# The last pair of a QKV projection done quad by quad, a later load of x, and casts of w on other engines

## The chip, the cores and the metric

The kernel runs on one core of one Trainium2 chip. The metric is the device time of one execution in microseconds (us), from before the first instruction to after the last store has landed; the time of a kernel is the median of its runs.

## The reference

One matrix product of fp32 matrices, split by columns into three outputs:

```
batch, seq, hidden = 16, 512, 768
qkv = np.matmul(x, w_qkv)            # (8192 x 768) @ (768 x 2304)
q, k, v = qkv[..., :hidden], qkv[..., hidden:2*hidden], qkv[..., 2*hidden:]
return np.stack([q, k, v], axis=0)   # 3 x 16 x 512 x 768, fp32
```

## The kernel before

**Pairs, quads and the remainder.** The 8192 rows of x are worked off in 32 pairs p of 2 x 128 rows. The 2304 columns of w are two groups q = 0, 1 of 1024 columns and 256 left over (`w_rem`). A quad (p, q) is an output tile `o` of 2 x 128 rows by 2 x 512 columns, that is four parts c11, c12, c21, c22 of 128 x 512. It is made by a scheme of seven block products instead of eight (Winograd's): products 1 and 2 are bf16 matmuls on the rounded x (`xb`) and `b1`, products 3 to 7 are matmuls on sums of x (`s`) and sums of w (`t`, `b22`). One product is three matmuls of 128 x 512. They go into three PSUM banks of the quad, x, y and z, and `do(u, n)` (L219) issues product n with what leaves the bank after it:

- 1 starts bank x, and ScalarE copies it to c11; 2 fills bank z, and VectorE adds it to c11.
- 6 adds onto bank x, ScalarE copies it to c12; 7 adds onto x, ScalarE copies it to c22; 4 adds onto x, ScalarE copies it to c21.
- 5 starts bank y; after 7, VectorE adds y to c22; 3 adds onto y, VectorE adds y to c12.

So products 6, 7 and 4 each add onto a bank that ScalarE must have read first, and product 3 onto one that VectorE must have read.

**Order.** The order on every engine is the program's own (`manual_schedule`). From pair 2 on, `two(a, b, early)` (L274) works on the two quads a and b of one pair in turn: a1 b1 a2 a6 b2 b6 a5 a7 b5 b7 a4, the remainder, b4 a3 b3, with stores of whole quads. `early` issues the next pair's transposition on VectorE (L123), its rounding (L174) and sums (L182 to L186) on GpSimd, and the load of x for the pair after that, half on SyncE's queue, half on ScalarE's. The last pair, p = 31, goes through `two_last` (L308): the same order, with stores by rows and parts, and the remainder's two rows at the very end, each copied by ScalarE (L333) and stored from ScalarE's queue (L335).

**The start.** x of pairs 0, 1 and 2 and all of w are loaded on SyncE's queue, in the order x0, `w_rem`, x1, w(0,0), x2, w(0,1), w(1,0), w(1,1), x3, where w(q,c) is the block of 512 columns c of group q and comes in two halves h of 3 x 512 per partition. Pairs 0 and 1 are done by plain bf16 matmuls: `rem(0)`, `rem(1)` and then `block(q, c, w, cast_next)` (L373), four blocks of 24 matmuls, each with its four PSUM banks copied by ScalarE (L390), and the casts of the next block's w issued by `cast_next` among these copies. Between `block(0, 0)` and `block(0, 1)` stand, for pair 2, the transposition by TensorE (L168), copies out of PSUM by VectorE (L138) and ScalarE (L139), the rounding and sums on GpSimd, and on VectorE the four sums of w for q = 0 (`sum_w`, L106) and a cast (L420). After the blocks VectorE makes the four sums for q = 1 (L427, again L106) and a cast (L428), and then the transposition for pair 3 (L123).

**Tiles that are used again.** The tag "big" has eight buffers for the `o` tiles and for the halves of w of q = 1. Quad (2, 1), quad b of the first pair in `two`, takes the buffer of the half (1, 0, 1) of w, which the last sum of q = 1 reads. Up to eight DMAs are under way at a time: each waits until the one eight before it, in the order of their issue, has landed.

Of the kernel before, what the change touches and what calls it, by code (L numbers as in the profile page):

```python
# [10 lines left out]
def kernel(  # L11
# [20 lines left out]
    nc = tc.nc  # L32
    P = 128
# [6 lines left out]
    KH = KT // 2  # L40
    KC = K // 4
    NP = M // (2 * P)
    CB = 512
    REM = N3 - 4 * CB
# [5 lines left out]
    ident = mybir.ActivationFunctionType.Identity  # L50
# [21 lines left out]
    b1 = [w_pool.tile([P, KT, CB], bf16, name=f"b1_{q}") for q in range(2)]  # L72
# [11 lines left out]
    stage = {}  # L84

    def load_blocks(q, c):
        if q == 0:
            t = tq_pool.tile([P, KT, CB], fp32, name="st0", tag="tq")
            for h in range(2):
                load_w(t[:, h * KH:(h + 1) * KH], h * KH, KH, Q_OFF[q] + c * CB, CB)  # L90
            stage[q, 0, c], stage[q, 1, c] = t[:, :KH, :], t[:, KH:, :]
        else:
            for h in range(2):
                t = big_pool.tile([P, KH, CB], fp32, name="st1", tag="big")
                load_w(t[:], h * KH, KH, Q_OFF[q] + c * CB, CB)
                stage[q, h, c] = t[:]
# [15 lines left out]
    def load_x(p, other):  # L112
        xin[p] = xin_pool.tile([P, 2 * P // G, KC], fp32, name="xin")
        t = xin[p]
        rows = x_flat[p * 2 * P:(p + 1) * 2 * P, :].rearrange("(g b) k -> b g k", b=G)
        for n in range(2):
            for h in range(2):
                i = 2 * h + n
                (nc.sync, other)[h].dma_start(t[i * G:(i + 1) * G], rows[:, :, i * KC:(i + 1) * KC])
# [52 lines left out]
    def round_x(p):  # L172
        xb[p] = xb_pool.tile([P, KT, 2 * P], bf16, name="xb")
        nc.gpsimd.tensor_copy(out=xb[p][:], in_=xf[p][:])  # L174
# [18 lines left out]
    def quad(p, q):  # L193
        u = Quad()
        u.p, u.q = p, q
        u.o = big_pool.tile([P, 2, 2 * CB], fp32, name="o", tag="big")
        u.x = u.y = u.z = None
        return u

    def product(u, n, ps, start):  # L200
        t1, t2, t3, t4 = ts[u.q]
        if n <= 2:
            h = (n - 1) * KH
            lhs = [xb[u.p][:, h + j, :P] for j in range(KH)]
            rhs = [b1[u.q][:, h + j, :] for j in range(KH)]
        else:
            k, t = {3: (4, b22[u.q][:]), 4: (0, t4), 5: (1, t1), 6: (2, t2), 7: (3, t3)}[n]
            lhs = [sr[u.p][:, k, j, :] for j in range(KH)]
            rhs = [t[:, j, :] for j in range(KH)]
        for j in range(KH):  # L210
            nc.tensor.matmul(  # L211
                ps[:], lhs[j], rhs[j],
                start=(start and j == 0), stop=(j == KH - 1), skip_group_check=True,
            )

    def bank():
        return ps_pool.tile([P, CB], fp32, name="ps")

    def do(u, n):  # L219
        c11, c12 = u.o[:, 0, :CB], u.o[:, 0, CB:]  # L220
        c21, c22 = u.o[:, 1, :CB], u.o[:, 1, CB:]
        if n == 1:
            u.x = bank()
            product(u, 1, u.x, True)
            nc.scalar.activation(c11, u.x[:], ident)  # L225
        elif n == 2:
            u.z = bank()
            product(u, 2, u.z, True)
            nc.vector.tensor_tensor(c11, c11, u.z[:], op=add)  # L229
        elif n == 6:  # L230
            product(u, 6, u.x, False)
            nc.scalar.activation(c12, u.x[:], ident)  # L232
        elif n == 5:
            u.y = bank()
            product(u, 5, u.y, True)
        elif n == 7:
            product(u, 7, u.x, False)
            nc.scalar.activation(c22, u.x[:], ident)  # L238
            nc.vector.tensor_tensor(c22, c22, u.y[:], op=add)  # L239
        elif n == 4:  # L240
            product(u, 4, u.x, False)
            nc.scalar.activation(c21, u.x[:], ident)  # L242
        elif n == 3:
            product(u, 3, u.y, False)
            nc.vector.tensor_tensor(c12, c12, u.y[:], op=add)  # L245
# [4 lines left out]
    def store_quad(u):  # L250
        if u.q == 0:
            nc.sync.dma_start(rows_of(0, u.p, 0, H), u.o[:, :, :H])
            nc.sync.dma_start(rows_of(1, u.p, 0, 2 * CB - H), u.o[:, :, H:])
        else:
            part = 2 * H - Q_OFF[1]
            nc.sync.dma_start(rows_of(1, u.p, H - part, H), u.o[:, :, :part])
            nc.sync.dma_start(rows_of(2, u.p, 0, H), u.o[:, :, part:])

    def rem_row(p, r, ps):
        for j in range(KT):  # L260
            nc.tensor.matmul(  # L261
                ps, xb[p][:, j, r * P:(r + 1) * P], w_rem[:, j, :],
                start=(j == 0), stop=(j == KT - 1), skip_group_check=True,
            )
# [30 lines left out]
    def store_cols(u, r, lo, hi, eng):  # L295

        c = Q_OFF[u.q] + lo
        end = Q_OFF[u.q] + hi
        while c < end:
            n = min(end, (c // H + 1) * H)  # L300
            row = (2 * u.p + r) * P
            eng.dma_start(
                out_flat[c // H, row:row + P, c % H:c % H + n - c],
                u.o[:, r, c - Q_OFF[u.q]:n - Q_OFF[u.q]],
            )
            c = n

    def two_last(a, b):  # L308

        do(a, 1)  # L310
        do(b, 1)
        do(a, 2)
        do(a, 6)
        do(b, 2)
        do(b, 6)
        do(a, 5)
        do(a, 7)
        do(b, 5)
        do(b, 7)
        store_cols(b, 0, 0, CB, nc.sync)  # L320
        do(a, 4)
        store_cols(a, 1, 0, 2 * CB, nc.sync)
        do(b, 4)
        store_cols(b, 1, 0, 2 * CB, nc.scalar)
        do(a, 3)
        store_cols(a, 0, 0, 2 * CB, nc.sync)
        do(b, 3)
        store_cols(b, 0, CB, 2 * CB, nc.sync)
        for r in range(2):
            ps = bank()  # L330
            rem_row(a.p, r, ps[:, :REM])
            o = or_pool.tile([P, 2, REM], fp32, name="orem")
            nc.scalar.activation(o[:, 0, :], ps[:, :REM], ident)  # L333
            row = (2 * a.p + r) * P
            nc.scalar.dma_start(out_flat[1, row:row + P, R_OFF - H:R_OFF - H + REM], o[:, 0, :])  # L335


    zero = w_pool.tile([P, CB], bf16, name="zero")
# [14 lines left out]
    o0 = [quad(p, 0) for p in range(2)]  # L353
    load_blocks(1, 0)
    load_blocks(1, 1)
    load_x(3, nc.sync)
    o1 = [quad(p, 1) for p in range(2)]

    def busy(n):
# [2 lines left out]
        for _ in range(n):  # L362
            nc.tensor.matmul(ps[:], zero[:, :P], zero[:], start=True, stop=True)

    def cast(q, h, c, w, eng):

        dst = w[:, h * KH:(h + 1) * KH, :]
        if eng is nc.scalar:
            eng.activation(dst, stage[q, h, c], ident)
        else:  # L370
            eng.tensor_copy(out=dst, in_=stage[q, h, c])

    def block(q, c, w, cast_next):  # L373


        ps = [bank() for _ in range(4)]
        for h in range(2):
            for n in range(4):
                p, r = divmod(n, 2)
                for j in range(h * KH, (h + 1) * KH):  # L380
                    nc.tensor.matmul(  # L381
                        ps[n][:], xb[p][:, j, r * P:(r + 1) * P], w[:, j, :],
                        start=(j == 0), stop=(j == KT - 1), skip_group_check=True,
                    )
                if h == 0:
                    continue
                if r == 0:
                    cast_next(p)
                o = (o0, o1)[q][p]
                nc.scalar.activation(o.o[:, r, c * CB:(c + 1) * CB], ps[n][:], ident)  # L390
                if c == 1 and r == 1:
                    store_quad(o)

    act, dve = nc.scalar, nc.vector
# [7 lines left out]
    rem(0)  # L402
    turn_bf16(1)
    rem(1)
    cast(0, 0, 0, b1[0], dve)
    cast(0, 1, 0, b1[0], dve)
    bt0 = bt_pool.tile([P, KT, CB], bf16, name="bt")
    bt1 = bt_pool.tile([P, KT, CB], bf16, name="bt")

    def cast_next(q, c, w):  # L410

        return lambda h: cast(q, h, c, w, act)

    block(0, 0, b1[0], cast_next(0, 1, bt0))
    turn_fp32(2)
    round_x(2)
    sums_x(2)
# [1 line left out]
        sum_w(0, n)  # L419
    dve.tensor_copy(out=b22[0][:], in_=stage[0, 1, 1])  # L420
    block(0, 1, bt0, cast_next(1, 0, b1[1]))
    block(1, 0, b1[1], cast_next(1, 1, bt1))
    block(1, 1, bt1, lambda h: None)
    t_1 = [tq_pool.tile([P, 2, KH, CB], f32r, name=f"t_1{n}", tag="tq") for n in range(2)]
# [5 lines left out]
    for p in range(2, NP):  # L430
        def early():
            if p + 1 < NP:
                transpose(p + 1)
                round_x(p + 1)
                sums_x(p + 1)
            if p + 2 < NP:
                load_x(p + 2, nc.scalar)

        if p < NP - 1:
            two(quad(p, 0), quad(p, 1), early)  # L440
        else:
            two_last(quad(p, 0), quad(p, 1))


# [28 lines left out]
```

## Time and profile before

| what | value |
|---|---|
| median of 4 runs (lowest to highest) | 369.63 us (369.53 to 369.74) |
| the profiled execution: its time | 369.58 us |
| its span, first to last instruction | 367.8 us |
| TensorE busy, share of the span | 359.0 us, 98% |
| VectorE, ScalarE, GpSimd busy | 62%, 51%, 50% |
| TensorE clock granted, mean | 0.997 |
| the chain that ended last, by engine | TensorE 90%, VectorE 4%, DMA 2%, issue 1%, ScalarE 1% |
| one pair in `two`, on that chain | 1.33 us remainder + 9.54 us quads |
| HBM traffic | 32.24 MB read, 75.50 MB written |

How to read it: "TensorE busy" counts matmuls whose ends are modelled, so what counts is not the 98% but the stretches in which a matmul waits. A timeline row gives the start, the duration, the engine (PE is TensorE, PEld its weight loads, DVE VectorE, ACT ScalarE, POOL GpSimd; a q behind it means the engine's queue, which issues DMAs), the line, the operation, the tiles out<-in and their shape, how many instructions are merged, and in brackets how long the engine stood idle before it and what ended that.

### The profile page before, as it was taken

What the parts mean: (1) busy time and instruction counts of PE and PEld (TensorE: products, weight loads), DVE (VectorE), ACT (ScalarE), POOL (GpSimd) and SP (SyncE); (2) the same over time, 40 slices, a digit from 0 to 9 for tenths busy, and PEclk for the clock granted to TensorE, in tenths of its full rate; (3) what the DMA queues carried; (4) which work ended last, traced back from release to release, by engine and by line L of the source; (5) the groups of instructions that cost most, each with busy time, mean ns of one, the idle gap of its engine ahead of it and who ended that gap; (6) DMA issues with size and microseconds to landing.
All of it is one profiled execution on the core that took longest, in us unless ns stands there. A gap on an engine that the chain in (4) does not pass through costs nothing.

```text
span 367.8 us, 5180 instructions
## 1 busy us (share of the span) xinstructions
PE 359.0 (98%) x1791; PEld 246.5 (67%) x1791; DVE 229.1 (62%) x233; ACT 186.1 (51%) x308; POOL 184.5 (50%) x188
## 2 busy tenths in 40 slices
PE   7999899999999999999999999999999999999994
PEld 3544667667766667776666776666777676677663
DVE  2399876655576665567665557666556766555732
ACT  4498444545544455454454554455545444445442
POOL 1049374456654356664445665444665544566510
PEclk9999999999999999999999999999999999999998
DMA  8999988888998888998888899988899888899776
GB/s 285 390 373 342 325 292 272 278 298 272 305 322 278 270 292 273 309 311 290 273 282 295 272 308 305 286 279 290 280 299 313 293 268 283 283 284 311 259 272 242
DMA packets 80122, 108.09 MB, mean 294 GB/s; under 512 B 4704, under 2 KB 59872, under 8 KB 80096
## 3 DMA queue, kind: packets, MB, share of 16 engines
q1 hardware_dynamic: 64288, 95.96, 79.4%
q10 hardware_dynamic: 15808, 11.80, 10.1%
q8 instruction: 14, 0.23, 0.3%
q14 instruction: 12, 0.10, 0.1%
HBM read 32.24 MB, written 75.50 MB: 293 GB/s over the span
## 4 chain that ended last, share of the span: by engine, by line
PE 90%; DVE 4%; DMA 2%; issue 1%; ACT 1%; SPq 0%; ACTq 0%; DVEq 0%
PE ps L211 77%; PE ps L261 11%; DVE t L106 3%; DMA xin<-in_x_dram 2%; PE ps L381 1%; DVE b L420 0%; PE ps L168 0%; PE ps L157 0%; ACT orem L333 0%; SPq L82 0%; ACT o L225 0%; ACT xc L139 0%; DVE xf L138 0%; SPq L134 0%; ACTq L335 0%
## 5 line engine op out<-in xcount | busy, mean ns | idle before, releaser
L211 PE MATMUL ps<-t,s 128*128 128x512 f32 x720 | 194.4, 412 | 1.2 <-ACT o L225 1.2
L211 PEld LDWEIGHTS ps<-t,s 128*128 128x128 f32 x720 | 133.1, 188 | 34.0 <-ACT o L225 1.7
L174 POOL CAST xb<-xf 128x1536 bf16<-128x1536 f32 x30 | 45.4, 1514 | 162.9 <-DVE xf L123 141.7
L123 DVE STREAM_TRANSPOSE xf<-xin 128x1536 f32<-128x1536 f32 x29 | 87.2, 3006 | 1.5 <-DMA xin<-in_x_dram 1.3
L211 PE MATMUL ps<-b,xb 128*128 128x512 bf16 x360 | 88.1, 381 | 0.0
L245 DVE TENSOR_TENSOR o<-o,ps 128x512 f32<-128x512 f32 x60 | 41.3, 688 | 61.5 <-PE ps L211 61.4
L239 DVE TENSOR_TENSOR o<-o,ps 128x512 f32<-128x512 f32 x60 | 41.2, 689 | 55.0 <-ACT o L238 55.0
L211 PEld LDWEIGHTS <-xb 128*128 128x128 bf16 x360 | 30.5, 98 | 44.5 <-issue 15.5
L238 ACT ACTIVATE o<-ps 128x512 f32<-128x512 f32 x60 | 36.0, 600 | 46.7 <-PE ps L211 46.7
L225 ACT ACTIVATE o<-ps 128x512 f32<-128x512 f32 x60 | 35.8, 597 | 46.3 <-PE ps L211 42.2
L232 ACT ACTIVATE o<-ps 128x512 f32<-128x512 f32 x60 | 35.8, 599 | 44.0 <-PE ps L211 43.3
L261 PE MATMUL ps<-w_rem,xb 128*128 128x256 bf16 x384 | 47.7, 273 | 0.5 <-DVE w_rem L400 0.4
L211 PE MATMUL ps<-b,s 128*128 128x512 f32 x180 | 46.5, 393 | 0.0
L261 PEld LDWEIGHTS <-xb 128*128 128x128 bf16 x384 | 34.9, 98 | 13.2 <-issue 8.9
L229 DVE TENSOR_TENSOR o<-o,ps 128x512 f32<-128x512 f32 x60 | 38.1, 683 | 2.0 <-PE ps L211 2.0
L211 PEld LDWEIGHTS ps<-b,s 128*128 128x128 f32 x180 | 33.8, 188 | 8.0
L242 ACT ACTIVATE o<-ps 128x512 f32<-128x512 f32 x60 | 35.9, 598 | 4.8 <-PE ps L211 0.4
L183 POOL TENSOR_TENSOR s<-s,xf 128x384 fp32r<-128x384 f32 x30 | 31.1, 1037 | 2.3
L186 POOL TENSOR_TENSOR s<-xf,s 128x384 fp32r<-128x384 f32 x30 | 32.1, 1070 | 0.0
L182 POOL TENSOR_TENSOR s<-xf 128x384 fp32r<-128x384 f32 x30 | 31.9, 1064 | 0.0
L184 POOL TENSOR_TENSOR s<-xf 128x384 fp32r<-128x384 f32 x30 | 31.7, 1058 | 0.0
L271 ACT ACTIVATE orem<-ps 128x512 f32<-128x512 f32 x31 | 18.6, 598 | 23.3 <-PE ps L261 23.3
(39 smaller groups left out, 115.2 us busy)
## 6 DMA issues: line engine op xcount, KB each, us to landing
out_dram<-o SPq DMA_DIRECT2D x62, 768.0 KB, 5.8
out_dram<-o SPq DMA_DIRECT2D x63, 256.0 KB, 4.7
xin<-in_x_dram SPq DMA_DIRECT2D x60, 192.0 KB, 6.7
xin<-in_x_dram ACTq DMA_DIRECT2D x56, 192.0 KB, 5.7
out_dram<-orem SPq DMA_DIRECT2D x31, 256.0 KB, 2.4
st<-in_w_qkv_dram SPq DMA_DIRECT2D x8, 768.0 KB, 13.9
xin<-in_x_dram SPq DMA_DIRECT2D x3, 768.0 KB, 7.4
str<-in_w_qkv_dram SPq DMA_DIRECT2D x1, 768.0 KB, 6.1
```

What stands on the lines that cost most here:

```text
L123: nc.vector.transpose(t[:].rearrange("p j (g b) -> p g j b", b=G), xin.pop(p)[:].rearrange("p g (a j) -> p g j a", a=G),)
L174: nc.gpsimd.tensor_copy(out=xb[p][:], in_=xf[p][:])
L186: g.tensor_tensor(s[:, 4], a12, s[:, 2], op=sub)
L211: nc.tensor.matmul(ps[:], lhs[j], rhs[j], start=(start and j == 0), stop=(j == KH - 1), skip_group_check=True,)
L225: nc.scalar.activation(c11, u.x[:], ident)
L229: nc.vector.tensor_tensor(c11, c11, u.z[:], op=add)
L232: nc.scalar.activation(c12, u.x[:], ident)
L238: nc.scalar.activation(c22, u.x[:], ident)
L239: nc.vector.tensor_tensor(c22, c22, u.y[:], op=add)
L242: nc.scalar.activation(c21, u.x[:], ident)
L245: nc.vector.tensor_tensor(c12, c12, u.y[:], op=add)
L261: nc.tensor.matmul(ps, xb[p][:, j, r * P:(r + 1) * P], w_rem[:, j, :], start=(j == 0), stop=(j == KT - 1), skip_group_check=True,)
```

## The change

It has four parts.

1. `two_last` is replaced by `last`: the two quads of pair 31 one behind the other, each as 1 2 6 5 7, one row of the remainder, 4 3, each part of `o` stored as soon as it is complete. The second row of the remainder stands inside quad b, so the last product is b3 and the last store the c12 part of b.
2. `load_x(3)`, four DMAs on SyncE's queue, moves from before the first stores to behind `block(0, 1)`, which issues the stores of the two q = 0 quads of pairs 0 and 1.
3. The cast of w(0,0) for `block(0, 0)`: of each half's three rows of 512, VectorE casts two and ScalarE the third, instead of VectorE all three.
4. The cast of the second half of w(0,1) for `block(0, 1)` moves from ScalarE to GpSimd, ahead of GpSimd's work for pair 2.

```
-    def two_last(a, b):
...
+    def last(a, b):
+        p = a.p
+        def rem_stored(r):
             ps = bank()
-            rem_row(a.p, r, ps[:, :REM])
+            rem_row(p, r, ps[:, :REM])
             o = or_pool.tile([P, 2, REM], fp32, name="orem")
             nc.scalar.activation(o[:, 0, :], ps[:, :REM], ident)
...
+        for r, u in enumerate((a, b)):
+            do(u, 1)
+            do(u, 2)
+            store_cols(u, 0, 0, CB, nc.sync)
+            do(u, 6)
+            do(u, 5)
+            do(u, 7)
+            rem_stored(r)
+            store_cols(u, 1, CB, 2 * CB, nc.sync)
+            do(u, 4)
+            store_cols(u, 1, 0, CB, nc.scalar)
+            do(u, 3)
+            store_cols(u, 0, CB, 2 * CB, nc.sync)
...
     load_blocks(1, 1)
-    load_x(3, nc.sync)
...
-    def cast(q, h, c, w, eng):
-        dst = w[:, h * KH:(h + 1) * KH, :]
+    def cast(q, h, c, w, eng, js=slice(0, KH)):
+        dst = w[:, h * KH + js.start:h * KH + js.stop, :]
+        src = stage[q, h, c][:, js, :]
...
     rem(1)
-    cast(0, 0, 0, b1[0], dve)
-    cast(0, 1, 0, b1[0], dve)
+    for h in range(2):
+        cast(0, h, 0, b1[0], dve, slice(0, 2))
+        cast(0, h, 0, b1[0], act, slice(2, KH))
...
-    block(0, 0, b1[0], cast_next(0, 1, bt0))
+    cast(0, 1, 1, bt0, nc.gpsimd)
+    block(0, 0, b1[0], lambda h: h == 0 and cast(0, 0, 1, bt0, act))
...
     block(0, 1, bt0, cast_next(1, 0, b1[1]))
+    load_x(3, nc.sync)
     block(1, 0, b1[1], cast_next(1, 1, bt1))
```

More of the change, by code (lines that the diff above doesn't have):

```diff
@@ L306, in store_cols @@
             c = n
-    def two_last(a, b):
[L310 to L329, printed above, removed]
+    def last(a, b):
+        p = a.p
+        def rem_stored(r):
             ps = bank()
-            rem_row(a.p, r, ps[:, :REM])
+            rem_row(p, r, ps[:, :REM])
             o = or_pool.tile([P, 2, REM], fp32, name="orem")
             nc.scalar.activation(o[:, 0, :], ps[:, :REM], ident)
-            row = (2 * a.p + r) * P
+            row = (2 * p + r) * P
             nc.scalar.dma_start(out_flat[1, row:row + P, R_OFF - H:R_OFF - H + REM], o[:, 0, :])
+        for r, u in enumerate((a, b)):
[11 more added lines that the diff above has]
+            store_cols(u, 0, CB, 2 * CB, nc.sync)
     zero = w_pool.tile([P, CB], bf16, name="zero")
@@ L363, in busy @@
             nc.tensor.matmul(ps[:], zero[:, :P], zero[:], start=True, stop=True)
-    def cast(q, h, c, w, eng):
-        dst = w[:, h * KH:(h + 1) * KH, :]
+    def cast(q, h, c, w, eng, js=slice(0, KH)):
+        dst = w[:, h * KH + js.start:h * KH + js.stop, :]
+        src = stage[q, h, c][:, js, :]
         if eng is nc.scalar:
-            eng.activation(dst, stage[q, h, c], ident)
+            eng.activation(dst, src, ident)
         else:
-            eng.tensor_copy(out=dst, in_=stage[q, h, c])
+            eng.tensor_copy(out=dst, in_=src)
     def block(q, c, w, cast_next):
@@ L441 @@
         else:
-            two_last(quad(p, 0), quad(p, 1))
+            last(quad(p, 0), quad(p, 1))
 _INS = ['x', 'w_qkv']
```

## The prediction

> **What bounds the kernel now.** I read the chain that ended last first. It is TensorE for 90% of the span, pair behind pair without a gap (1.33 + 9.54 us each); all that isn't TensorE lies in the first 40 us and the last 5. Here it is around the only long wait of the matmuls:
>
> ```profile
> 36.12 2.56 DVE t L106
> ...
> 38.70 0.04 ACTq L225
> ...
> 38.78 0.61 ACT o L225
> ...
> 39.43 4.41 PE ps L211 x18
> 43.84 1.33 PE ps L261 x12
> ```
>
> VectorE's last sum of w (L106) ends at 38.67; only then may ScalarE write c11 of quad b of pair 2, and only then may product b6 add onto that bank. So two things set the start: TensorE's own stream from 10.9 to 38.2, and VectorE's row of sums, which begins when TensorE has transposed x of pair 2. The timeline of the start:
>
> ```profile
> 12.41 5.34 PE L381 MATMUL ps<-b,xb 128*128 128x512 bf16 x24
> 12.62 0.60 ACT L271 ACTIVATE orem<-ps 128x512 f32<-128x512 f32 x1 [0.83 <-PE ps L261]
> 13.40 0.96 DVE L371 CAST b<-st 128x1536 bf16<-128x1536 f32 x1 [1.07 <-DMA st<-in_w_qkv_dram]
> ...
> 17.39 1.48 ACT L369 ACTIVATE bt<-st 128x1536 bf16<-128x1536 f32 x1 [4.18 <-DMA st<-in_w_qkv_dram]
> ...
> 18.98 0.56 DVE L138 COPY xf<-ps 128x384 f32<-128x384 f32 x1 [0.25 <-PE ps L168]
> ...
> 23.03 2.96 POOL L174 CAST xb<-xf 128x1536 bf16<-128x1536 f32 x1 [21.21 <-DVE t L106]
> ...
> 24.58 3.02 DVE L106 TENSOR_TENSOR t<-st,t 128x1536 fp32r<-128x1536 f32 x1
> ...
> 38.78 0.60 ACT L225 ACTIVATE o<-ps 128x512 f32<-128x512 f32 x1 [2.55 <-DVE t L106]
> ...
> 39.43 4.41 PE L211 MATMUL ps<-t,s 128*128 128x512 f32 x18 [1.23 <-ACT o L225]
> 39.46 3.12 DVE L123 STREAM_TRANSPOSE xf<-xin 128x1536 f32<-128x1536 f32 x1
> ```
>
> To be seen: block(0, 0) runs from 12.41 at 0.216 us a matmul ((5.34 - 0.38) / 23) without waiting, since VectorE's cast was done at 12.33; ScalarE is at that moment tied to the remainder's copy, 12.62 to 13.22; VectorE stands idle before 18.98 for TensorE; and a sum takes 1.75 us alone (the three before 24.58) but 2.05 to 3.02 while GpSimd works. The end:
>
> ```profile
> 358.51 0.60 ACT L238 ACTIVATE o<-ps 128x512 f32<-128x512 f32 x1 [0.77 <-PE ps L211]
> ...
> 359.16 0.53 PEld L211 LDWEIGHTS ps<-t,s 128*128 128x128 f32 x3 [0.42 <-ACT o L238]
> ...
> 363.02 0.38 ACT L333 ACTIVATE orem<-ps 128x256 f32<-128x256 f32 x1 [0.42 <-PE ps L261]
> 363.44 0.45 ACTq L335 DMA_DIRECT2D out_dram<-orem  x1
> ```
>
> ```profile
> DMA to landing us min/median/max: 2.1/3.2/4.2
> ```
>
> The second fence is the view of L302, the last pair's stores. At 359.16 product b4 waits for the copy of b7's bank although a4 stands between them: one product does not cover one copy. The last matmul ends at 362.84, the last store (L335, 3.0 to 3.4 us to landing) lands about 366.8, the span ends at 367.8, about 0.96 later.
>
> **Part 3, a third of the first casts on ScalarE.** In the built order ScalarE's new cast stands behind the remainder's copy of rem(1) and TensorE's third matmul of block(0, 0) waits for it. That matmul was due at 12.41 + 2 x 0.216 = 12.84. ScalarE is free at 13.22 (successive ScalarE copies overlap by about 0.1, so 13.12). The profile has no 128x512 cast there; 128x768 is 0.83 (L399) and 128x1536 1.48, 0.85 ns an element, so 0.83 - 256 x 0.85 ns = 0.61; bounds 0.51 (the 128x384 row of L139) and 0.83. The cast ends at 13.73 and TensorE stands still for 13.73 - 12.84 = **0.9 us** (0.8 to 1.1). What VectorE saves (0.32 a cast) is worth nothing: it lay under rem(1) and in an idle stretch. The second half's third, done by about 14.3, is due at 12.84 + 0.9 + 10 x 0.216 = 15.9: covered. Nothing takes the 0.9 back: TensorE has no gap until 38.2, and the gap there is VectorE's row, which starts behind TensorE's transposition and moves by the same 0.9.
>
> **Part 4, the cast on GpSimd.** ScalarE loses 1.48 at 19.74, so its copies for pair 2 end about 1.3 earlier and GpSimd's rounding and sums begin at about 21.7 instead of 23.03. That buys nothing: no matmul waits for them (the sums serve products from 36.5 on; the last is done at 37.06, needed near 46). The halves of w land 2.0 us apart (the waits end at 11.37 and 13.40, then 17.39 two transfers later), so this one lands near 19.4; the cast takes 1.51 (mean of L174), to 20.9; block(0, 1) needs it at 19.18 + 0.9 + 12 x 0.216 = 22.7: covered by 1.8. But VectorE's first sum, due at 19.45 + 0.9 = 20.35, meets it. In the trace the sum at 24.58 is held until GpSimd's cast ends at 25.99, 1.27 more than its 1.75. So I charge the overlap, 20.9 - 20.35 = **0.5** (0 when it lands earlier or does not hold VectorE; 2.0 when the cast takes the 2.96 of its own row). GpSimd's other six operations stretched VectorE's row by 1.27 + 0.81 + 0.80 + 0.69 + 0.30 + 0.80 = 4.7; all six fall inside the row in both kernels: 0, give or take one (0.8).
>
> The note in the Trainium skill, "Advanced Engine Details and Errata", section Mode Summary, says that GpSimd and two-port Vector instructions block each other; its own table gives a tensor_tensor no two-port mode, so by it the 0.5 would be 0 and the sum 0.5 lower. The row at 24.58 is a tensor_tensor that was stretched; the row decides.
>
> **Part 2, x of pair 3.** SyncE's queue issued its four pieces from 17.23 to 23.81; now the two remainder stores go out there and the pieces follow the four q = 0 stores. From the landing of the last w on (30.45, where L369's wait for it ends) there are 0.5 MB remainder, 2.1 MB stores and 0.8 MB x to move; at the 374 to 408 GB/s of the windows between 30 and 42 that is 3.4 MB / 0.39 = 8.7 us: x lands near 39.1. VectorE turns to it (L123) at 39.46 + 1.4 = 40.9. Cover 1.7; behind it, pair 3's first product starts some 3.4 after the remainder at 43.68, at 47.1, and the rounding ends at 44.12, another 3.0. Price 0; a transfer later than 4.7 us would cost its excess. The following loads wait in part for each other across two queues, with the same cover.
>
> **Part 1, the end.** Matmuls are the same in number. In each quad 6, 7 and 4 now follow the copy of their bank with one product (or half a remainder, 6 x 0.11) between. From the last matmul of a product: 0.39 to its end, 0.04, copy 0.60, 0.05, and 0.10 for the weights that could not be preloaded, 1.18; covered by four slots of 0.23 = 0.91, so 0.27, as at 359.16. Six such waits less the one that was there: 6 x 0.28 - 0.25 = +1.4; bounds 0 (hidden) and 1.9. Product 3 waits for VectorE's add, which just fits (0.1). So the last matmul ends at 362.84 + 1.4 = 364.25. Behind it VectorE's add 0.69 + 0.07, and one 256 KB store in place of a copy and a 128 KB store: 2.4 to landing, near the minimum of 2.1 because fewer are in flight (up to 3.4). That is 3.2 against 4.0 before. Net **+0.6** (-1.1 to +2.1). ScalarE's stores stand behind their own copies and are issued before the next copy is due.
>
> The Trainium skill, "DMA: Bandwidth & Descriptors", Anatomy of one DMA, fits 2.0 us + bytes / 436e3 for a DMA issued by GpSimd. By that estimate the 256 KB would take 2.6, and the sum would be 0.2 higher; the rows stay.
>
> **Sum.** 0.9 + 0.5 + 0 + 0.6 = +2.0 on the profiled 369.58 (span 367.8, 1.78 around it; 0.05 under the median of 369.63): **371.6**.
>
> **Rivals.**
> - *The start costs more*: GpSimd's cast lands or runs late and holds VectorE's row 2.0 instead of 0.5, or x of pair 3 comes after all cover. For it: 2.96 for the same cast, 7 to 8 us landings under load. Against: it would run with VectorE idle. 373.1.
> - *The start costs little*: ScalarE gets to its third early, or VectorE's row is stretched once less (-0.8). 370.6 to 370.8. Against: the copy it stands behind ends at 13.22.
> - *The end wins* (the other side): bank waits vanish in TensorE's queue and the last store lands in 2.1. The last matmul ends at 362.6, then 0.76 + 2.1 + 0.96: 366.4, -1.4. With the start at 1.4 that is 369.6; it turns faster than before by more than 0.2% once the start costs under 0.7. Against: the wait at 359.16 is just this case.
> - *It doesn't do what it says*: ScalarE in fact gains two casts of a third and loses one whole; that is part of the sum.
>
> **How the numbers follow.** 0.2%, 0.74 us, is about what a measurement of this kernel can tell from no change. Forecast 0.63 (its own range 370.8 to 372.6); start costs more 0.13; start costs little 0.10, a fifth of it within 0.2% by a better end; the end wins 0.10, half of it faster, half within 0.2%; 0.04 for what I have not seen, half to each of these two. So faster 0.07, same 0.09, slower 0.84. The range, 370.1 to 373.1, takes in the forecast and most of the two rivals at the start and leaves out the end's win and GpSimd or x later still, under 2 in 10.
>
> **What would show it.** Right: the third matmul of block(0, 0) starts near 13.75 behind ScalarE's L366; GpSimd's L368 at 19.4; the last sum of q = 1 ends near 40.1 and b6 starts near 40.8; weight loads idle about 0.4 behind L232, L238 and again L238 in both quads of the last pair; the last store lands about 3.2 behind the last matmul. Wrong: no gap at 12.84, or VectorE's row starting at 19.45 as before.

## The result, and the profile after

The kernel after takes 370.23 us, median of 35 runs (370.06 to 371.67); the kernel before, run beside it, 369.62 us, median of 56 (369.46 to 371.08). The ratio is 1.0018 with a 95% interval of 1.0011 to 1.0025: +0.6 us, 0.18%. It is slower than before, but by less than the 0.2% that were named as the bound of a measurable difference, and by a third of the +2.0 that were predicted.

In a part of the executions of most kernels here, the one before included (its times lie at 369.5 to 369.8 or at 370.3 to 371.1), the loads of `w_rem` and of x of pair 1 land about 1.1 us later and everything behind them shifts with them; the profiled execution after is such a one (371.37 us, span 369.6). Its chain begins with a load of x of 8.47 us where that of before has 7.37. So traces are compared here from the first matmul of the remainder (L261, 7.98 us before, 9.10 after), which waits for `w_rem`:

| from the trace, us | before | after |
|---|---|---|
| first remainder to the remainder of pair 2 (the start) | 35.70 | 35.69 |
| from there to the remainder of pair 3, and of each later pair | 10.87, 10.87 | 10.95, 10.87 |
| remainder of pair 30 to the end of the last matmul | 14.71 | 16.43 |
| end of the last matmul to the end of the span | 4.95 | 3.83 |
| first remainder to the end of the span | 359.81 | 360.48 |

The sum is +0.67. Of it +0.07 lie at the start and +0.60 at the end; the prediction had +1.4 and +0.6. So the end came out as forecast, and the question is where the 1.4 of the start went.

The chain of waits after, around the start (start, duration, what; subtract 1.1 to compare with before):

```profile
1.95 8.47 DMA xin<-in_x_dram
...
13.72 0.60 ACT orem L271
14.32 0.53 ACT b L366
...
14.89 4.91 PE ps L378 x22
...
37.57 1.76 DVE t L106
...
39.43 0.42 ACT o L225
...
39.89 1.26 ACTq L119
...
41.19 0.61 ACT o L232
```

The first half is as forecast: TensorE's third matmul of block(0, 0) waits at 14.89, behind ScalarE's third cast (L366), which stands behind the remainder's copy (L271). The second half is not. At 39.43 the copy of c11 for quad b (L225) starts when a sum of w ends at 39.32, and that sum began at 37.57. The timeline says which one it is:

```profile
14.89 4.91 PE L378 MATMUL ps<-b,xb 128*128 128x512 bf16 x22 [0.77 <-ACT b L366]
...
20.56 1.46 POOL L368 CAST bt<-st 128x1536 bf16<-128x1536 f32 x1 [18.74 <-DMA st<-in_w_qkv_dram]
...
21.49 2.14 DVE L106 TENSOR_TENSOR t<-st,st 128x1536 fp32r<-128x1536 f32 x1
...
37.56 1.75 DVE L106 TENSOR_TENSOR t<-st,st 128x1536 fp32r<-128x1536 f32 x1
...
39.23 1.75 DVE L106 TENSOR_TENSOR t<-st,t 128x1536 fp32r<-128x1536 f32 x1
...
39.43 0.60 ACT L225 ACTIVATE o<-ps 128x512 f32<-128x512 f32 x1 [1.17 <-DVE t L106]
...
40.08 1.65 PE L211 MATMUL ps<-t,s 128*128 128x512 f32 x6
...
41.77 3.09 DVE L123 STREAM_TRANSPOSE xf<-xin 128x1536 f32<-128x1536 f32 x1
```

Two sums stand there. The copy at 39.43 does not wait for the last one (39.23 to 40.98), but for the third (ended 39.31). Before, it waited for the last (36.12 to 38.67, copy at 38.78). The last sum does come later, 40.98 - 1.12 - 38.67 = 1.2; product b6 (the row at 40.08) comes earlier than before, 40.08 - 1.12 - 39.43 = -0.5. What follows gives this back: the second of the two loads of x that ScalarE issues there (L119) takes 1.26 us to issue, 0.71 before, so its next copy (L232) comes only at 41.19, and the remainder of pair 2 starts where it did before.

The end after, first the weight loads of the last pair (PEld), then the view of its stores (L302):

```profile
354.30 1.23 PEld L211 LDWEIGHTS ps<-t,s 128*128 128x128 f32 x6 [0.59 <-issue]
356.02 0.54 PEld L211 LDWEIGHTS ps<-t,s 128*128 128x128 f32 x3 [0.48 <-issue]
...
357.73 0.53 PEld L211 LDWEIGHTS ps<-t,s 128*128 128x128 f32 x3 [0.36 <-issue]
...
360.77 1.23 PEld L211 LDWEIGHTS ps<-t,s 128*128 128x128 f32 x6 [0.53 <-ACT o L225]
362.42 0.53 PEld L211 LDWEIGHTS ps<-t,s 128*128 128x128 f32 x3 [0.43 <-ACT o L232]
...
364.08 0.53 PEld L211 LDWEIGHTS ps<-t,s 128*128 128x128 f32 x3 [0.29 <-ACT o L238]
```

```profile
DMA to landing us min/median/max: 1.7/2.4/4.4
```

The weight loads stand idle 0.29 to 0.59 ahead of products 6, 7 and 4 in both quads, behind ScalarE's copies L225, L232 and L238 in turn. Ahead of quad a's three products the records call the idle time "issue", but the rows start 0.11 us behind the end of the same copies (in quad b 0.05). The stores land after a median of 2.4 us instead of 3.2; the last one, issued at 366.51, lands after 2.13.

### The profile page after: what moved, and what is told of

It reads as the page before. It is cut to its first block, busy times and chain, and to the rows that moved or that the text cites. A ratio compares the mean times of both kernels' runs of the same rounds, so it can differ in the third digit from the quotient of the medians.

```text
span 369.6 us, 5190 instructions
## 1 busy us (share of the span) xinstructions
PE 360.7 (98%) x1791; PEld 245.9 (67%) x1791; DVE 228.9 (62%) x233; ACT 186.3 (50%) x309; POOL 185.2 (50%) x189
## 3 DMA queue, kind: packets, MB, share of 16 engines
q10 hardware_dynamic: 15952, 11.80, 10.4%
## 4 chain that ended last, share of the span: by engine, by line
PE 94%; DMA 2%; ACT 1%; DVE 1%; ACTq 0%; SPq 0%; issue 0%
PE ps L211 77%; PE ps L261 11%; PE ps L378 6%; DMA xin<-in_x_dram 2%; DVE t L106 0%; PE ps L168 0%; ACTq L119 0%; PE ps L157 0%; DVE o L245 0%; SPq L82 0%; ACT o L232 0%; ACT o L387 0%; ACT orem L271 0%; ACT xc L139 0%; ACT b L366 0%
## 5 line engine op out<-in xcount | busy, mean ns | idle before, releaser
L238 ACT ACTIVATE o<-ps 128x512 f32<-128x512 f32 x60 | 36.0, 600 | 47.3 <-PE ps L211 47.3
L225 ACT ACTIVATE o<-ps 128x512 f32<-128x512 f32 x60 | 35.8, 597 | 45.7 <-PE ps L211 40.1
L232 ACT ACTIVATE o<-ps 128x512 f32<-128x512 f32 x60 | 35.8, 599 | 45.3 <-PE ps L211 45.3
L261 PE MATMUL ps<-w_rem,xb 128*128 128x256 bf16 x384 | 47.8, 273 | 1.7 <-DVE w_rem L397 1.6
L261 PEld LDWEIGHTS <-xb 128*128 128x128 bf16 x384 | 34.9, 98 | 14.5 <-issue 10.3
L183 POOL TENSOR_TENSOR s<-s,xf 128x384 fp32r<-128x384 f32 x30 | 31.9, 1064 | 2.4
L271 ACT ACTIVATE orem<-ps 128x512 f32<-128x512 f32 x31 | 18.5, 598 | 23.3 <-PE ps L261 23.3
```

The costliest lines, as they stand in the source:

```text
L261: nc.tensor.matmul(ps, xb[p][:, j, r * P:(r + 1) * P], w_rem[:, j, :], start=(j == 0), stop=(j == KT - 1), skip_group_check=True,)
```

## The experiments

Each kernel was timed beside the kernel before on the same chip; "on the trace" is the stretch from the first remainder to the end of the span, against 359.81.

**The parts one by one.** Four kernels: the kernel before with part 3 alone (e1), with part 4 alone (e2), with both (e3), and with part 1 alone (e4). Their edits are those pieces of the diff above.

e1:

> The kernel before with part 3 alone (a third of the first two casts on ScalarE). Theory B (the buffer decides: quad b of pair 2 takes over the buffer of a half of w, and its first copy waits for the last sum that reads it, the fourth of q = 1 here): TensorE stands 0.9 us at the third matmul of block(0, 0), VectorE's row and the fourth sum come 0.9 later, nothing takes it back: +0.9 us (370.5; 0.7 to 1.1). Rival A (the stop at the start is absorbed at 38 whatever the buffer is, so that nothing of the start ever counts): 0.0 (369.6).

e2:

> The kernel before with part 4 alone (the second half of block(0, 1) cast by GpSimd). VectorE's first sum is due at 19.45 there, 0.9 earlier than in the kernel after, and GpSimd's cast runs from 19.4 to 20.9, so that the sum is held by up to 1.3 (as the sum at 24.58 was). Theory B (copy of quad b waits for the fourth sum): +1.2 us (370.8; 0.9 to 1.4). Rival A (absorbed): 0.0 (369.6).

e3:

> The kernel before with parts 3 and 4 together. Theory B: with both in, quad b of pair 2 stands in the buffer of another half of w, whose last reader is the third sum of q = 1; the third ends about 1.75 before the fourth, so the 0.9 + 0.4 of the start is taken back but for some 0.1: 0.0 us (369.6; -0.2 to +0.2), less than either part alone. Rival C (each part adds its own price, as the prediction summed them): +1.3 us (370.9). Rival A: 0.0, but then the two kernels with one part each are at 0.0 too.

e4:

> The kernel before with part 1 alone (the last pair's quads one behind the other). By the prediction's term and by the trace of the kernel after: the last matmul comes 1.4 to 1.7 later, the chain behind it is 1.1 shorter: +0.6 us (370.2; 0.4 to 0.8), all of the kernel's difference. Rival D (the difference of the two kernels lies at the start or in the loads of x, and the end is even): 0.0 (369.6).

| | median us (lowest) | before us (lowest) | ratio, 95% interval | start, us | on the trace |
|---|---|---|---|---|---|
| e1, part 3 | 370.52 (370.43) | 369.70 (369.47) | 1.0018, 1.0007 to 1.0028 | 36.66 | +0.89 |
| e2, part 4 | 371.07 (370.75) | 369.70 (369.47) | 1.0054, 1.0035 to 1.0073 | 36.94 | +1.24 |
| e3, both | 369.88 (369.47) | 369.70 (369.47) | 1.0007, 0.9998 to 1.0016 | 35.71 | +0.12 |
| e4, part 1 | 370.23 (370.19) | 369.70 (369.47) | 1.0018, 1.0008 to 1.0027 | 35.74 | +0.65 |

Part 3 costs 0.9 alone and part 4 costs 1.2 alone, but both together cost 0.1. That rules out that the prices add up (rival C), and that the start absorbs such costs anyhow (rival A). In e2's timeline GpSimd's cast holds VectorE's first sum for 3.06 - 1.75 = 1.31, and the copy of quad b still waits for the last sum:

```profile
19.38 1.46 POOL L372 CAST bt<-st 128x1536 bf16<-128x1536 f32 x1 [17.57 <-DMA st<-in_w_qkv_dram]
19.41 3.06 DVE L106 TENSOR_TENSOR t<-st,st 128x1536 fp32r<-128x1536 f32 x1
...
38.06 1.75 DVE L106 TENSOR_TENSOR t<-st,t 128x1536 fp32r<-128x1536 f32 x1
...
39.92 0.60 ACT L225 ACTIVATE o<-ps 128x512 f32<-128x512 f32 x1 [3.43 <-DVE t L106]
```

In e3's, the copy starts at 38.51, when the third sum is done, while the last one runs on to 40.06:

```profile
36.65 1.75 DVE L106 TENSOR_TENSOR t<-st,st 128x1536 fp32r<-128x1536 f32 x1
...
38.31 1.75 DVE L106 TENSOR_TENSOR t<-st,t 128x1536 fp32r<-128x1536 f32 x1
...
38.51 0.60 ACT L225 ACTIVATE o<-ps 128x512 f32<-128x512 f32 x1 [1.19 <-DVE t L106]
```

What the sums read (`sum_w`) says why. Name a half of w by (q, c, h): the half (1, 0, 1), in the code `stage[1, 1, 0]`, is read last by the fourth sum, and the half (1, 1, 0), in the code `stage[1, 0, 1]`, by the third. In the kernel before, in e1, e2 and e4 the copy waits for the fourth sum, so quad b's `o` tile stands in the buffer of (1, 0, 1); in e3 and in the kernel after it waits for the third, so the tile stands in that of (1, 1, 0). No line of the diff says so: the planner that hands out the eight "big" buffers picks another one once both casts are moved. Why it does was not tried. e4 has the whole difference of the kernel after at the end, +0.65 of +0.67.

**The wait put back, and taken away.** e6 and e9 are the kernel after with one more reader of the buffer that quad b takes there (`stage[1, 0, 1]`), so that quad b waits for the fourth sum again; e6 reads into a new tile, e9 into one that exists. e7 is the kernel before with the last two sums in the other order, so that the reader of quad b's buffer comes third.

```
e6: after the four sums of q = 1
+    touch = w_pool.tile([P, 1], fp32, name="touch")
+    nc.vector.tensor_copy(out=touch[:], in_=stage[1, 0, 1][:, 0, :1])
e9: after the four sums of q = 1
+    nc.vector.tensor_copy(out=zero[:, :1], in_=stage[1, 0, 1][:, 0, :1])
e7: the sums of q = 1
-    for n in range(1, 5):
+    for n in (1, 2, 4, 3):
         sum_w(1, n)
```

e6:

> The kernel after with one more reader of the buffer that quad b of pair 2 now takes: a copy of one element a partition on VectorE, about 0.1 us, behind the fourth sum of q = 1, so that quad b's first copy waits for the fourth sum again. Theory B (the buffer takes the start's cost back): the fourth sum ends about 1.2 later than in the kernel before, net of the loads, so +1.2 us on the kernel after, +1.8 on the kernel before (371.4; 371.0 to 371.7), near what was predicted. Rival A (the cost is absorbed whatever quad b waits for): as the kernel after, +0.6 on the kernel before (370.2).

e7:

> The kernel before with the last two sums of q = 1 in the other order (1, 2, 4, 3): quad b of pair 2 still takes the same buffer, but its last reader is now the third sum in VectorE's order, done some 1.75 earlier. Theory B: the 1.23 us for which TensorE stands at 38.2 falls to 0.2 or to nothing, -1.0 to -1.2 us (368.5). Rival E (TensorE stands there for something else, or the wait comes back further on): 0.0 (369.6).

e6 took 373.91 us (372.73 to 374.00; before 370.09; ratio 1.0088, 1.0069 to 1.0107), twice what the theory gave. Its start is 36.98, +1.29 on the kernel after, as expected; but each of its pairs takes 10.92 instead of 10.87, and 28 of these are the other 1.3. e9 and e10 were made to tell whether that comes from the wait or from the new tile, which by the program's layout moves every later tile by 32 bytes (the traces show no addresses). e10 is the kernel before with the two lines of e6, where no wait changes by them.

e9:

> The kernel after with the added reader of e6, but its one element a partition goes into an existing tile (the zeros of the opening matmuls, not read any more), so that every tile lies at the address that it has in the kernel after; in e6 a new tile had moved the later ones by 32 bytes, and each pair took 10.92 us there in place of 10.87. Theory B with the 0.05 a pair put down to the move: the second remainder starts 36.9 to 37.0 behind the first one (35.69 in the kernel after), pairs take 10.87, so +1.2 us on the kernel after (371.4; 371.1 to 371.7). Rival G (the later wait itself makes the pairs slower): pairs 10.92, 372.7. Rival A (absorbed): 370.2.

e10:

> The kernel before with the new one-element tile and the copy of e6, in a place where no wait changes by it (quad b of pair 2 waits for the fourth sum with and without it). If moving the later tiles by 32 bytes slows the matmuls: pairs 10.92, 28 x 0.05 = +1.4 us (371.0). If not: 10.87 and 0.0 to +0.1 (369.6).

e9: start 36.91, pairs 10.87, on the trace 361.64, that is +1.16 on the kernel after. Its times are 371.32 to 372.88, median 372.46, ratio to before 1.0054 (1.0035 to 1.0074); five of its seven runs are 1.0 to 1.6 above the lowest, much as late loads make them, so the size is read from the trace. Its rows show the wait that was put back, with the added copy (L428) in front of it:

```profile
38.04 1.75 DVE L106 TENSOR_TENSOR t<-st,t 128x1536 fp32r<-128x1536 f32 x1
...
39.71 0.14 DVE L428 CAST zero<-st 128x1 bf16<-128x1 f32 x1
...
39.90 0.60 ACT L225 ACTIVATE o<-ps 128x512 f32<-128x512 f32 x1 [2.84 <-DVE zero L428]
...
40.55 4.41 PE L211 MATMUL ps<-t,s 128*128 128x512 f32 x18 [1.50 <-ACT o L225]
```

So with the old wait the kernel after costs about +1.8 on the trace, near the +2.0 of the prediction: the buffer alone takes back 1.2. e10: pairs 10.92, +1.45 on the trace, 372.02 us (371.00 to 372.45), ratio 1.0049 (1.0032 to 1.0067). So one more small tile costs 1.3 us in the pairs by itself. That this is the address of the other tiles, and what in it slows the matmuls, was not tried.

e7: 369.21 us (368.44 to 369.94; before 370.09, lowest 369.56), ratio 0.9973 (0.9959 to 0.9988), on the trace -1.16. Quad b's copy no longer stands in the way, and TensorE runs through the place where it had waited 1.23:

```profile
36.15 2.56 DVE L106 TENSOR_TENSOR t<-st,st 128x1536 fp32r<-128x1536 f32 x1
...
37.87 4.50 PE L211 MATMUL ps<-t,s 128*128 128x512 f32 x18
```

The start falls by 1.50 (to 34.20), and 0.36 comes back in the next pair (11.23 instead of 10.87). Rival E falls, but for this 0.36.

**Part 2 alone** (e5: `load_x(3)` moved, nothing else):

> The kernel before with part 2 alone (x of pair 3 loaded behind the first stores). Theory and prediction: it lands by about 39, VectorE turns to it at 40.9 or later: 0.0 us (369.6; -0.2 to +0.2). Rival: it or the loads queued behind it come late and hold a pair: +0.5 or more.

On the trace +0.09 (start 35.75, pairs 10.87). The times are 370.96 us, median of 12 (370.01 to 371.55), against 370.09, median of 29, ratio 1.0017 (1.0005 to 1.0029). Ten of the twelve are as high as late loads make them, against about half of before's; the other two are 0.4 above before's lowest. So the price is 0.1 by the trace and 0.4 to 0.6 by the times, and the two were not reconciled. In the kernel after there is no room for 0.4: e4, which has no part 2, has the same time and the same trace to 0.02.

**The end, done otherwise.** In e8 the quads stay interleaved and the remainder comes between a4 and b4; in e11 the order is a4, a3, b4, remainder, b3; e13 is e11 with each part stored as it ends, and with SyncE issuing all of these stores. (The expectation of e11 says that e11 stores by parts too; its edit still stores both rows of a and the second row of b whole.) e12 and e14 add the swapped sums of e7 to e11 and e13. The core of them:

```
e8: remainder and b4 change places; stores
+        store_cols(a, 0, 0, CB, nc.sync)          (behind b7)
-        store_cols(b, 1, 0, 2 * CB, nc.scalar)
-        store_cols(a, 0, 0, 2 * CB, nc.sync)
+        store_cols(b, 1, 0, 2 * CB, nc.sync)      (behind b4)
+        store_cols(a, 0, CB, 2 * CB, nc.scalar)   (behind a3)
e11
-        do(b, 4)
-        store_cols(b, 1, 0, 2 * CB, nc.scalar)
         do(a, 3)
         store_cols(a, 0, 0, 2 * CB, nc.sync)
+        do(b, 4)
+        store_cols(b, 1, 0, 2 * CB, nc.scalar)
-        do(b, 3)
-        store_cols(b, 0, CB, 2 * CB, nc.sync)
         for r in range(2):
             ...
+        do(b, 3)
+        store_cols(b, 0, CB, 2 * CB, nc.sync)
e13, e11 with these stores for its own: behind products 2, 7, 4 and 3 of each quad u
+        store_cols(u, 0, 0, CB, nc.sync)
+        store_cols(u, 1, CB, 2 * CB, nc.sync)
+        store_cols(u, 1, 0, CB, nc.sync)
+        store_cols(u, 0, CB, 2 * CB, nc.sync)
```

e8:

> The kernel before with the end done in another way: the quads of the last pair interleaved as they were, the remainder's two rows between a's and b's product 4 in place of behind everything, a's c11 stored as soon as it is done and only its c12 on ScalarE's queue. Theory: no bank wait is added (the interleaved products cover the copies), the 0.25 wait of product b4 is covered by the remainder, and the last chain is an add and a 256 KB store (0.76 + 2.1 + 0.96 = 3.8) in place of 4.95: -1.1 to -1.3 us (368.4). Rival F (the last chain is bound by the bytes in flight, so that the order of the end matters little): 0.0 to -0.4.

e11:

> The kernel before with the order of the end a4, a3, b4, remainder, b3, each part stored as it ends: a3 lies between b7 and b4, so that the wait of 0.25 is covered, and the last product's 256 KB store is the only one issued in the last 1.5 us. In e8 the last store took 3.15 to land beside four others issued within 1.1 us; in the kernel after it took 2.13 alone. Theory (the spacing of the last stores sets the end): last matmul -0.25, chain behind it 3.9 to 4.4 in place of 4.95: -0.8 to -1.3 us (368.6). Rival F (the stores before it hold it as they did in e8): -0.3 (369.3).

e12:

> The kernel before with the two edits that gained nothing from the change: the last two sums of q = 1 in the other order (e7, -1.1 by its start) and the end of e11. If the two add up: -1.9 to -2.4 us (367.5; 367.2 to 367.8). If the end gives only 0.3: 368.2.

e13:

> The kernel before with the order of e11 (a4, a3, b4, remainder, b3) and, as in the kernel after, each part of a quad stored as soon as it is done (c11 behind product 2, c22 behind 7, c21 behind 4, c12 behind 3), all of them by SyncE, so that ScalarE's queue has the remainder's two stores alone. In e8 and e11 the last store was issued 0.7 to 1.1 earlier against the last matmul than in the kernel before and landed no earlier: from the first store of a's second row on, some 1.5 MB stood in the queues. Theory H (the bytes still to be stored when the last product ends set the end, so the gain of 1.1 behind the last matmul in the kernel after comes from storing parts early, not from the order of the quads): here some 0.4 MB are left then, the last store lands in 2.1 to 2.5, the chain behind the last matmul is 3.85 to 4.3: -0.9 to -1.3 us (368.5). Rival I (the gain of the kernel after needs one quad behind the other, so that the stores of a are through before those of b): again 0.0 to -0.3 (369.4).

e14:

> e13 with the last two sums of q = 1 in the other order (e7). By theory H both gains add up: -2.0 to -2.4 us (367.4). By rival I as e12: -1.1 (368.4).

| | median us (lowest) | before us (lowest) | ratio, 95% interval | last pair, us | behind the last matmul | on the trace |
|---|---|---|---|---|---|---|
| before | | | | 14.71 | 4.95 | |
| after | | | | 16.43 | 3.83 | +0.67 |
| e8 | 370.42 (369.35) | 370.09 (369.56) | 1.0001, 0.9988 to 1.0013 | 14.44 | 4.80 | -0.39 |
| e11 | 369.71 (369.56) | 370.43 (369.47) | 1.0001, 0.9985 to 1.0018 | 14.46 | 5.16 | +0.04 |
| e12 | 369.58 (368.31) | 370.43 (369.47) | 0.9972, 0.9954 to 0.9989 | 14.46 | 5.18 | -1.15 |
| e13 | 368.36 (368.26) | 369.67 (369.56) | 0.9967, 0.9955 to 0.9979 | 14.46 | 3.90 | -1.24 |
| e14 | 367.05 (367.04) | 369.67 (369.56) | 0.9927, 0.9915 to 0.9940 | 14.46 | 3.90 | -2.46 |

All five lose the bank wait of 0.25, as expected. But e8 and e11 missed what was expected behind the last matmul, and so e12 has the gain of e7 alone. The store of b's c12 is issued 0.75 us behind the last matmul in e8, e11, e13 and the kernel after alike. It lands in 3.15 us in e8 and 3.10 in e11, but in 2.13 in the kernel after and 2.21 in e13. (Before, the last store is a row of the remainder, issued 0.60 behind the last matmul and landing in 3.39; so, other than e13's expectation has it, e8 and e11 did not issue their last store earlier. Nor was the last store of the kernel after alone: three others were under way.) What differs is what is still to land: at the end of the last matmul, stores of 1.6 MB before, 1.4 in e8 and 1.6 in e11, but 0.9 in the kernel after and 1.0 in e13. The view by windows shows when they could have been stored (PE, PEld, DVE, ACT, POOL busy, the clock, DMA share, GB/s); e11, then e13:

```profile
358.00:361.00 3.00, 3.00 (x18) 2.27 (x17) 1.85 (x3) 1.58 (x3) 0.00 (x0) 1.00 0.43 157
361.00:364.00 3.00, 1.61 (x12) 1.06 (x9) 0.69 (x1) 0.98 (x3) 0.00 (x0) 1.00 1.02 373
```

```profile
358.00:361.00 3.00, 3.00 (x18) 2.27 (x17) 1.82 (x3) 1.61 (x3) 0.00 (x0) 1.00 0.92 325
361.00:364.00 3.00, 1.58 (x12) 1.03 (x9) 0.69 (x1) 0.95 (x3) 0.00 (x0) 1.00 1.03 353
```

In e11 the DMA engines stand half idle from 358 to 361 (157 GB/s; before, 158), and are full from 361 to 364: what could have been stored in the first window waits for its row to be complete and is then in the way of the last store. In e13 the first window carries 325 GB/s.

e11 is also held by something else. ScalarE issues the two stores of b's second row from 361.25 to 362.54 and copies the remainder only then, so the store that lands last is a row of the remainder, issued 1.25 behind the last matmul and landing 0.35 after c12. In e13 SyncE has those stores. So of the 1.26 between the two, about 0.35 is ScalarE's queue and 0.9 the quicker landing of c12; no run parts the two changes on this order of products. That the quicker landing does not need SyncE's queue is seen in the kernel after, where ScalarE issues c21 of both quads and c12 lands in 2.13.

So theory H holds: it is the early storing of parts that makes the chain behind the last matmul 1.1 shorter in the kernel after, and the order of the quads only costs. e13 has the order that adds no bank wait and the storing that frees the queues, and e14 with the swapped sums beats both kernels: 367.05 us, 0.7% under before, and every one of its five runs is under 367.2.

## Why the prediction was wrong

Step by step:

- **Part 3, TensorE stands 0.9 at the third matmul: right.** 14.89 less the 1.12 of the loads is 13.77; forecast 13.75. Alone it costs 0.89 on the trace (e1). The new cast takes 0.62, forecast 0.61.
- **"Nothing takes the 0.9 back": this step failed.** It stood on "the gap there is VectorE's row, which starts behind TensorE's transposition and moves by the same 0.9". The row did move, its last sum by 1.2. But the gap was never tied to the whole row. It was tied to the sum that last reads the buffer of quad b, and that was the fourth sum before and is the third after. I had named the buffer and its reader in the kernel before, and took both to hold in the kernel after. Net of the loads, the last sum ends there at 39.86, near the 40.1 forecast, but b6 starts at 38.96 and not at 40.8. So the start cost 0.07 and not 1.4. With the old wait put back the same kernel costs 1.2 more (e9).
- **Part 4, 0.5: the mechanism right, the term slightly large.** GpSimd's cast starts at 20.56 - 1.12 = 19.44 (forecast 19.4) and takes 1.46 (1.51). It holds the first sum 2.14 - 1.75 = 0.4. Alone, where the sum is due 0.9 earlier, it holds it 1.3, and costs 1.24 (e2). The section Mode Summary of "Advanced Engine Details and Errata" in the Trainium skill, read as excluding a tensor_tensor from this, would have given 0; the rows show 0.4 and 1.3.
- **Part 2, 0: right on the trace** (0.09 in e5; the 0.4 to 0.6 of e5's times stay open). In the kernel after VectorE turns to x of pair 3 at 41.77 without a wait.
- **Part 1, the end +0.6: right in the sum, with both terms too small.** The bank waits cost 16.43 - 14.71 = 1.72 (forecast 1.4): by the starts of the matmuls the six waits are 0.27 to 0.38 each (forecast 0.28), the three of quad a the longer, since the weight loads start there 0.11 behind the copy and not 0.05. The chain behind the last matmul is 4.95 - 3.83 = 1.12 shorter (forecast 0.8), since the last store took 2.13 and not 2.4. The estimate from the Trainium skill, "DMA: Bandwidth & Descriptors", section Anatomy of one DMA, which fits a DMA issued by GpSimd, was 2.6; this store, issued by SyncE, lies below it.

The sum as measured: 0.9 + 0.4 - 1.2 (the buffer) = 0.1 at the start, 0.6 at the end, +0.7. Of the rivals, *the start costs little* (370.6 to 370.8) came nearest, but the start cost less still, and by none of the ways named for it: ScalarE got to its third no earlier, and VectorE's row was stretched no less (19.2 us from the first sum's start to the last one's end before, 19.5 after). That the sum at the end came out at +0.6 is in part luck: its two terms were off by 0.3 each, in opposite directions.

## What to carry to other kernels

In a program like this one, where tiles share buffers, a write waits for the last reader of the buffer it was given, and an edit far away can give it another one: compare which instruction each wait names in both built programs before pricing a delay, and order the readers of a shared buffer so that the one needed first is read first (e7: -1.2 us for one swapped pair). In a kernel that ends in stores like this one, store each part as soon as it is complete, and judge the end by the bytes still to land when the last product ends, not by the issue time of the last store (e11 against e13: c12, issued at the same distance, lands in 2.2 instead of 3.1). Look also at what else stands on the queue that issues the last stores. Give a new small tile its place with care: one ahead of the others cost 1.3 us here.

## What was not expected of the hardware

- One more small tile, with the same instructions in the pairs, made their fp32 matmuls slower: 10.92 us a pair instead of 10.87, in e6 and e10 alike. In the groups of e10 the mean of the `t`,`s` matmuls is 413 ns, before 412, and of the `b`,`s` matmuls 396, before 393; the bf16 ones have 380 and 381. Spread over 54 matmuls a pair this is too small to be seen in single rows. That it comes from moving the tiles by 32 bytes is inferred.
- The load of x of pair 1 lands at 9.3 us after the span's start in the trace before and at 10.4 in the trace after, and the whole execution is longer by the difference; x of pair 0 is there at 5.1 in both. What makes the loads late was not tried.
- A VectorE sum of 1.75 us that begins with a GpSimd cast of 1.46 is held for almost all of it (3.06, e2); one that begins 0.9 later in the cast is held for 0.4 (2.14).
